# Columns of sc1 and sh1 as one-column products of w_ada's blocks with silu(c)

## The chip, the core and the metric

The kernel runs on one core of a Trainium2 chip. Its time is the device time of one execution in microseconds (us), median of three runs. A core has five engines that run side by side, each working through its own queue in order: PE (matrix products; the load of the stationary operand is shown apart as PEld), DVE (vector), ACT (scalar, activations), POOL and SP, which here only issues DMAs. PE's clock has two levels, 1.2 and 2.4 GHz; the profile shows the granted clock as a share of the higher one.

## What is computed

One layer of a decoder trunk over 2048 tokens of 1024 channels, in float32. The part that the change touches is the modulation at the head of the layer:

```
c_act = silu(c)                                  # 1024 values
mod = c_act @ w_ada[l] + b_ada[l]                # [1024] x [1024, 6144]
sh1, sc1, g1, sh2, sc2, g2 = split(mod, 6)
h = rmsnorm(x, norm_mix_in[l]) * (1.0 + sc1) + sh1
proj = h @ w_in[l]                               # then attention, pooling, gating
```

Everything after it (attention in windows, pooling, spatial gating, output projection and a SwiGLU FFN) depends on h, and so on sc1 and sh1, which take 2 x 1024 columns of w_ada, 8 MB.

## The kernel before

The 2048 tokens go in four groups of 512. Products that need more than the short format of one pass are made of a high and a low part, three passes each (`mm3`, lines of `L90`). Plain float32 operands go through `mm` (also L90), and the compiler makes two instruction pairs (weight load and product) of each such call.

`start()` handles group 0. It normalizes the four token tiles (L379), turns them into channels by transposes on PE (`turn`, L384), and forms sc1 and sh1 by quarters of 256 channels, since w_ada arrives by quarters: `loads(q)` (L399) issues four DMAs of 512 KB for a quarter, two for sh1 (j = 0) and two for sc1 (j = 1), each with 4 of the 8 blocks of 128 input channels. All 16 loads are issued ahead; between them stand the first three strips of w_in (L269). For each quarter:

- DVE makes the weighted sum of the eight blocks for sc1 into `acc` (one L434 and seven L436, each reading a column of `cact`, which is silu(c));
- ACT scales the eight blocks of sh1 in place (L441), POOL adds them up in four steps (L443 to L446);
- PE sums both over the 128 partitions by products with a column of ones: four calls of `mm`, two blocks of 128 channels for each of the two sums, eight instruction pairs;
- DVE adds the bias and forms A = (1 + sc1) * norm and the shift (L453 to L455) from the PSUM tile `aux`, of which there is one buffer;
- ACT applies them to the transposed tokens (L298), DVE splits the result into high and low part (L300, L301), and this is `hT[kc]`, for the two blocks of 128 channels of that quarter;
- PE transposes of quarter q + 2 (they reuse the PSUM banks that L298 has read), and the products of all strips so far with all `hT` so far (`first[j]`, three strips, 72 passes in all).

The block from the weighted sums to `hT` stands under `hp()`, which gives its instructions the priority of instructions 400 places earlier. The order of each engine's queue is set ahead of the run by the planner of the tile framework from priorities and from a timeline that it simulates; on the chip each queue then goes strictly in that order. After `start()`, `proj_a` evicts `first[0..2]` (L489), stores them (L490) and goes on with the rest of the projections; SP's queue carries these stores, the further strips (L269), further w_ada loads (L166) and the tokens of the next group (L148) in one order. Tiles of tag `b` (21 buffers) hold the 16 w_ada tiles, then `hT`; `raw` has 3 buffers, `hl` 4.

Of the kernel before, what the change touches and what calls it, by code (L numbers as in the profile page):

```python
# [12 lines left out]
AF = mybir.ActivationFunctionType  # L13
ALU = mybir.AluOpType

P = 128
T = 2048
D = 1024
KC = D // P
# [17 lines left out]
def tile_hybrid_trunk(  # L37
# [22 lines left out]
    PE, ACT, DVE, POOL, SP = nc.tensor, nc.scalar, nc.vector, nc.gpsimd, nc.sync  # L60
# [27 lines left out]

    def mm(ps, lhsT, rhs, start=True, stop=True):
        PE.matmul(ps, lhsT=lhsT, rhs=rhs, start=start, stop=stop)  # L90

# [8 lines left out]

# [1 line left out]
    q_s = dram.tile([NH * HD, T], F32, name="q_s")  # L102
# [5 lines left out]

# [1 line left out]
    ident = ct("ident", [P, P])  # L110
    make_identity(nc, ident)
    ones = ct("ones", [P, P])
# [18 lines left out]
    def sig_tail(y, e):  # L131
        """e <- log(1 + exp(-|y|)); y <- min(y, 0) - e; y <- exp(y) = sigmoid(y)."""
        ACT.activation(out=e, in_=y, func=AF.Abs)
        ACT.activation(out=e, in_=e, func=AF.Exp, scale=-1.0)
        ACT.activation(out=e, in_=e, func=AF.Ln, bias=1.0)
        DVE.scalar_tensor_tensor(out=y, in0=y, scalar=0.0, in1=e, op0=ALU.min, op1=ALU.subtract)
        ACT.activation(out=y, in_=y, func=AF.Exp)

    cact = ct("cact", [P, 8])
# [15 lines left out]
    r0 = 0  # L155
# [6 lines left out]

# [1 line left out]
    def ada_load(j, k):  # L164
# [55 lines left out]

# [1 line left out]
    sgn = ct("sgn", [P, 256])  # L222
# [28 lines left out]

# [1 line left out]
    cnt = [0]  # L253

    def wsplit(raw, hl):
        """hl[:, 0] + hl[:, 1] = raw, exactly."""
        n = raw.shape[1] * raw.shape[2]
        cnt[0] += 1
        r = raw.rearrange("p a b -> p (a b)")
        h = hl[:, 0].rearrange("p a b -> p (a b)")  # L260
        l = hl[:, 1].rearrange("p a b -> p (a b)")
        with hp():
            ACT.activation(out=h, in_=r, func=AF.Copy)  # L263
            eng = POOL if cnt[0] % 3 == 0 else DVE
            eng.tensor_tensor(out=l, in0=r, in1=h.bitcast(F32), op=ALU.subtract)  # L265
# [38 lines left out]
    def to_channels(xts, A, sh, res):  # L304
        """4 tiles [128 tok, 1024] -> 8 tiles [128 ch, hi/lo, 512 tok] of A * x + sh."""
        pss = {}
        for kc in range(KC):
            with hp():
                if kc % 3 == 2:
                    ps = aux()  # L310
                elif kc % 3 == 0:
                    zt = zps()
                    ps = zt[:, 0]
                else:
                    ps = zt[:, 1]
                for t in range(4):
                    PE.transpose(
                        out=ps[:, t * P : (t + 1) * P], in_=xts[t][:, kc * P : (kc + 1) * P], identity=ident
                    )
                pss[kc] = ps  # L320
                last = [kc] if kc % 3 == 2 else ([kc - 1, kc] if kc % 3 == 1 else [])
                for k in last:
                    res.append(modulate(pss[k], A, sh, k))
            yield

    def ws_unit(ps, hl, hT):
        """weight-stationary: ps[128 out ch, 512 tok]."""
        for kc in range(KC):
            mm3(
                ps, (hl[:, 0, kc, :], hl[:, 1, kc, :]), (hT[kc][:, 0], hT[kc][:, 1]), 0, 0, kc == 0, kc == KC - 1  # L330
            )

    def seg_scale(raws, dim):
        """1/rms over the channels of raws (tiles [128 ch, 512]), on every partition."""
        sqs = []
        for r in raws:
            sq = st("t2", [P, 512])
            ACT.activation(out=sq, in_=r, func=AF.Square)
            sqs.append(sq)
            if len(sqs) == 2:  # L340
                POOL.tensor_tensor(out=sqs[0], in0=sqs[0], in1=sqs[1], op=ALU.add)
                sqs.pop()
        ps = aux()
        mm(ps, ones, sqs[0])
        rs = st("t2", [P, 512])
        ACT.activation(out=rs, in_=ps, func=AF.Ln, scale=1.0 / dim, bias=epst)
        ACT.activation(out=rs, in_=rs, func=AF.Exp, scale=-0.5)
        return rs
# [7 lines left out]

# [1 line left out]
    hTs = {}  # L358
# [13 lines left out]
    first = []  # L372

    def start():
        """h of group 0 and its first products, as sc1 and sh1 become known by quarters of the channels."""
        xts = xt0
# [17 lines left out]
        def loads(q):  # L394
            res = {}
            for j in (0, 1):
                for hf in range(2):
                    wt = st("b", [P, 4, 256])
                    SP.dma_start(  # L399
                        out=wt,  # L400
                        in_=w_ada[0, hf * 512 : (hf + 1) * 512, j * D + q * 256 : j * D + (q + 1) * 256].rearrange(
                            "(k p) c -> p k c", p=P
                        ),
                    )
                    res[j, hf] = wt
            return res
# [10 lines left out]
        raws = []  # L417
# [9 lines left out]
        for q in range(4):  # L427
            w = wq.pop(q)
            with hp():
                acc = w[1, 0][:, 0, :]  # L430
                for k in range(KC):
                    wt = w[1, k // 4][:, k % 4, :]
                    if k == 0:
                        DVE.tensor_scalar(out=acc, in0=wt, scalar1=cact[:, 0:1], scalar2=None, op0=ALU.mult)  # L434
                    else:
                        DVE.scalar_tensor_tensor(  # L436
                            out=acc, in0=wt, scalar=cact[:, k : k + 1], in1=acc, op0=ALU.mult, op1=ALU.add
                        )
                for k in range(KC):
                    wt = w[0, k // 4][:, k % 4, :]  # L440
                    ACT.activation(out=wt, in_=wt, func=AF.Copy, scale=cact[:, k : k + 1])  # L441
                a0, a1 = w[0, 0], w[0, 1]
                POOL.tensor_tensor(out=a0[:, 0:2], in0=a0[:, 0:2], in1=a0[:, 2:4], op=ALU.add)  # L443
                POOL.tensor_tensor(out=a1[:, 0:2], in0=a1[:, 0:2], in1=a1[:, 2:4], op=ALU.add)
                POOL.tensor_tensor(out=a0[:, 0:2], in0=a0[:, 0:2], in1=a1[:, 0:2], op=ALU.add)
                POOL.tensor_tensor(out=a0[:, 0], in0=a0[:, 0], in1=a0[:, 1], op=ALU.add)  # L446
                ps = aux()
                for i, s in enumerate((acc, a0[:, 0])):
                    for cb in range(2):
                        mm(ps[:, 2 * i + cb : 2 * i + cb + 1], s[:, cb * P : (cb + 1) * P], ones[:, 0:1])  # L450
                qs = slice(2 * q, 2 * q + 2)
# [25 lines left out]
    def proj_a(g):  # L477
        tok = slice(g * GT, (g + 1) * GT)
        hT = hTs[g]
        # q, k  # L480
        for j in range(4):
# [10 lines left out]
        for j in range(4):  # L492
# [11 lines left out]
            yield 5.2  # L504
        # v
        for vb in range(2):
            hls = [strip(w_in[0], 1024 + vb * 256, 256, 4 * u, 4) for u in range(2)]
            for tp in range(2):
# [23 lines left out]
                yield 5.2  # L532
        # pooling
        praw = []
# [41 lines left out]

# [1 line left out]
    def proj_b(g, ga):  # L578
# [83 lines left out]

# [1 line left out]
    def att_front(g, h, i, qst, kst, koff):  # L664
        """weights of stick breaking of q tile i (of group g): [128 q, keys]."""
        nk = 5 if g > 0 else i + 1
# [45 lines left out]
    def att_back(g, i0, wq, vst, av):  # L712
        """av[:, pair] += [v_hi | v_lo]^T w^T for q tiles i0, i0 + 1."""
        if g > 0:
# [95 lines left out]

# [1 line left out]
    mTs = {}  # L812
# [35 lines left out]
    def tok_gemm(acts, w, r0, nk, gain, x1):  # L848
        """x1 += gain * (acts^T w[r0 : r0 + nk * 128]); acts: nk tiles [128, hi/lo, 512 tok]."""
        for hf in range(2):  # L850
# [70 lines left out]
    def down(g):  # L921
        f0, n, acts = ACTS.pop(0)
        yield from tok_gemm(acts, w_down[0], f0 * P, n, M["g2"], X1[g])

    def down_last(g):
        """the last part of down() with the final norm of each token tile right after it."""
        f0, n, acts = ACTS.pop(0)
# [59 lines left out]

# [1 line left out]
    att = attention()  # L989
# [14 lines left out]
    def weave(fg, *sides):  # L1004
        """emit fg; each side (generator, first tick, steps per tick[, last tick]) goes along."""
        live = [[e[0], e[1], e[2], 0.0, e[3] if len(e) > 3 else 1000] for e in sides]
# [103 lines left out]
```

## Time and profile before

| | |
|---|---|
| time, median of 3 runs | 2464.58 us (2461.14 to 2466.43) |
| span of the profiled execution | 2463.7 us, 32486 instructions |
| PE busy | 2352.7 us, 95% |
| weight loads (PEld) busy | 1977.3 us, 80% |
| DVE, ACT, POOL busy | 1692.1 (69%), 1362.9 (55%), 1217.0 us (49%) |
| mean granted clock of PE | 0.986 |

The profile gives the profiled execution's span, from its first to its last instruction; its own time is not given apart from the three runs. "Busy" is the time in which an engine has an instruction under way; products overlap one another, so the duration of one is longer than the distance from one start to the next. Times in rows count from the span's start.

### The profile page before, as it was taken

The numbers are of one execution on the slowest core, as the hardware profiler recorded it, in microseconds if no ns is written. First come the engines' busy times: TensorE is split into PE (matmuls) and PEld (weight loads), VectorE is DVE, ScalarE is ACT, GpSimd is POOL, SyncE is SP. The second block draws the span as 40 slices with busy tenths as digits, with TensorE's granted clock in tenths as the row PEclk, the third lists the DMA queues.
The fourth block names the chain that finished last, engine by engine and source line by source line (L and its number), as shares of the span: only waits on it lengthen the run. The fifth ranks groups of instructions, "written<-read, shape, count | busy, mean of one in ns | idle before, by whom it ended". The sixth has DMA issues, their size and how long they took to land.

```text
span 2463.7 us, 32486 instructions
## 1 busy us (share of the span) xinstructions
PE 2352.7 (95%) x11730; PEld 1977.3 (80%) x11730; DVE 1692.1 (69%) x2125; ACT 1362.9 (55%) x2307; POOL 1217.0 (49%) x1157
## 2 busy tenths in 40 slices
PE   5999999999999999998999999889999999999998
PEld 4888979788788888777888888768788878788887
DVE  7577888767876777878877777877775456543435
ACT  5366767656666655656665655566664343433333
POOL 4142533345465455675554555754554456344445
PEclk8999999999999999999999999999999999999999
DMA  8857374554333333433433334334333343433332
GB/s 250 270 167 238 120 244 133 158 165 122 96 97 105 105 104 98 139 121 100 129 115 105 105 102 132 124 98 130 99 103 90 102 146 102 140 95 99 98 100 77
DMA packets 336512, 315.62 MB, mean 128 GB/s; under 512 B 12168, under 2 KB 267870, under 8 KB 336352
## 3 DMA queue, kind: packets, MB, share of 16 engines
q1 hardware_dynamic: 336352, 313.56, 41.3%
q8 instruction: 92, 1.51, 0.2%
q14 instruction: 68, 0.56, 0.1%
HBM read 279.95 MB, written 33.56 MB: 127 GB/s over the span
## 4 chain that ended last, share of the span: by engine, by line
PE 49%; DVE 18%; POOL 11%; issue 10%; ACT 8%; DMA 4%; SPq 1%; POOLq 0%; DVEq 0%; ACTq 0%
PE d L90 45%; POOL b L868 4%; DVE ee L704 3%; DVE hl L265 2%; DVE zc L707 2%; POOL hl L265 2%; PE av L90 2%; ACT hl L263 1%; DMA qst<-q_s 1%; DVE b L301 1%; PE tr L735 1%; DMA b<-in_w_ada_dram 1%; PE z L90 1%; DVE ee L690 1%; POOL b L916 1%
## 5 line engine op out<-in xcount | busy, mean ns | idle before, releaser
L90 PE MATMUL d<-b,hl 128*128 128x512 f32 x5184 | 1254.2, 395 | 8.3 <-DVE b L300 3.2
L90 PEld LDWEIGHTS d<-b,hl 128*128 128x128 f32 x5184 | 961.9, 189 | 208.2 <-DVE b L300 5.0
L90 PE MATMUL d<-hl,b 128*128 128x512 f32 (+1 forms) x4428 | 913.9, 359 | 13.2 <-DVE y L867 12.4
L90 PEld LDWEIGHTS d<-hl,b 128*128 128x128 f32 x4428 | 728.9, 191 | 128.3 <-DVE y L867 15.0
L263 ACT ACTIVATE hl<-raw 128x1024 fp32r<-128x1024 f32 x368 | 387.1, 1054 | 238.0 <-PE d L90 231.0
L265 POOL TENSOR_TENSOR hl<-raw,hl 128x1024 fp32r<-128x1024 f32 x122 | 308.2, 2527 | 325.1 <-ACT hl L263 308.7
L265 DVE TENSOR_TENSOR hl<-raw,hl 128x1024 fp32r<-128x1024 f32 x246 | 336.1, 1368 | 191.9 <-ACT hl L263 185.0
L868 POOL TENSOR_TENSOR b<-b,y 128x512 f32<-128x512 f32 x248 | 388.8, 1576 | 143.4 <-DVE y L867 135.8
L916 POOL TENSOR_TENSOR b<-y,b 128x512 fp32r<-128x512 f32 x88 | 165.0, 1875 | 228.3 <-DVE b L915 223.0
L704 DVE TENSOR_TENSOR_SCAN ee<-ee 128x640 f32<-128x640 f32 (+4 forms) x128 | 204.5, 1598 | 61.8 <-POOL ee L698 54.8
L867 DVE TENSOR_TENSOR y<-d,b 128x512 f32<-128x512 f32 x248 | 167.7, 681 | 91.4 <-PE d L90 88.9
L709 ACT ACTIVATE zc<-zc 128x640 f32<-128x640 f32 (+4 forms) x128 | 85.8, 670 | 257.5 <-POOL zc L698 223.4
L90 PE MATMUL av<-wT,vst 128*128 128x256 f32 x672 | 173.0, 295 | 30.6 <-DVE wT L751 13.4
L693 POOL TENSOR_SCALAR_AFFINE_SELECT zc<-zc 128x128 f32<-128x128 f32 x128 | 81.4, 636 | 221.9 <-DVE zc L707 213.8
L751 DVE TENSOR_TENSOR wT<-tr,wT 128x128 fp32r<-128x128 f32 (+1 forms) x280 | 116.6, 416 | 85.5 <-ACT wT L750 85.2
L90 PEld LDWEIGHTS av<-wT,vst 128*128 128x128 f32 x672 | 122.5, 192 | 59.7 <-DVE wT L751 21.4
L750 ACT ACTIVATE wT<-tr 128x128 fp32r<-128x128 f32 (+1 forms) x280 | 105.8, 378 | 104.4 <-DVE wT L751 71.2
L690 DVE SCALAR_TENSOR_TENSOR ee<-zc,ee 128x640 f32<-128x640 f32 (+4 forms) x128 | 125.5, 981 | 47.9 <-ACT ee L688 47.2
L693 POOL TENSOR_SCALAR_AFFINE_SELECT ee<-ee 128x128 f32<-128x128 f32 x128 | 53.6, 419 | 193.2 <-DVE ee L690 189.6
L907 ACT ACTIVATE y<-d 128x512 f32<-128x512 f32 x88 | 52.3, 594 | 150.8 <-PE d L90 150.7
L707 DVE TENSOR_TENSOR zc<-zc,ee 128x640 f32<-128x640 f32 (+4 forms) x128 | 133.7, 1044 | 2.4
L910 DVE SCALAR_TENSOR_TENSOR y<-d,y 128x512 f32<-128x512 f32 x88 | 60.3, 685 | 84.1 <-ACT y L909 83.7
(187 smaller groups left out, 2248.1 us busy)
## 6 DMA issues: line engine op xcount, KB each, us to landing
raw<-in_w_gate_up_dram SPq DMA_DIRECT2D x176, 512.0 KB, 3.9
raw<-in_w_down_dram SPq DMA_DIRECT2D x88, 512.0 KB, 3.7
raw<-in_w_in_dram SPq DMA_DIRECT2D x72, 512.0 KB, 5.2
b<-in_w_ada_dram SPq DMA_DIRECT2D x48, 512.0 KB, 6.7
raw<-in_w_out_dram SPq DMA_DIRECT2D x32, 512.0 KB, 4.3
b<-in_x_dram SPq DMA_DIRECT2D x28, 512.0 KB, 6.0
kst<-k_s SPq DMA_DIRECT2D x24, 512.0 KB, 4.1
qst<-q_s SPq DMA_DIRECT2D x64, 128.0 KB, 4.3
```

Source lines behind the costliest of these rows:

```text
L90: PE.matmul(ps, lhsT=lhsT, rhs=rhs, start=start, stop=stop)
L263: ACT.activation(out=h, in_=r, func=AF.Copy)
L265: eng.tensor_tensor(out=l, in0=r, in1=h.bitcast(F32), op=ALU.subtract)
L690: DVE.scalar_tensor_tensor(out=sp, in0=zc, scalar=0.0, in1=e, op0=ALU.max, op1=ALU.add)
L693: POOL.affine_select(out=t[:, n - P : n], in_=t[:, n - P : n], pattern=[[-1, P]], compare_op=ALU.is_ge, fill=fill, base=-1, channel_multip ...
L704: DVE.tensor_tensor_scan(out=e[:, ::-1], data0=sp[:, ::-1], data1=sp[:, ::-1], initial=0.0, op0=ALU.add, op1=ALU.bypass)
L707: DVE.tensor_tensor(out=zc, in0=zc, in1=e, op=ALU.subtract)
L750: ACT.activation(out=wT[:, 0, a:b], in_=tr[:, a:b], func=AF.Copy)
L751: DVE.tensor_tensor(out=wT[:, 1, a:b], in0=tr[:, a:b], in1=wT[:, 0, a:b].bitcast(F32), op=ALU.subtract)
L867: DVE.tensor_tensor(out=y, in0=ps, in1=gain[:, cs], op=ALU.mult)
L868: POOL.tensor_tensor(out=x1[t][:, cs], in0=x1[t][:, cs], in1=y, op=ALU.add)
L916: POOL.tensor_tensor(out=a[:, 1], in0=y, in1=a[:, 0].bitcast(F32), op=ALU.subtract)
```

## The change

In place of the weighted sums, PE multiplies each block of w_ada itself (as the stationary operand, 128 input channels by 128 columns) with the matching column of silu(c): per quarter 2 halves x 2 parts x 4 blocks x 2 column blocks = 32 calls of `mm`, all summed in PSUM as one accumulation group over four columns of `aux`. The sums on DVE, ACT and POOL go, and so do the products with ones. The loads of a quarter are issued by halves of the input channels, sc1 first.

```diff
-    def mm(ps, lhsT, rhs, start=True, stop=True):
-        PE.matmul(ps, lhsT=lhsT, rhs=rhs, start=start, stop=stop)
+    def mm(ps, lhsT, rhs, start=True, stop=True, skip=False):
+        PE.matmul(ps, lhsT=lhsT, rhs=rhs, start=start, stop=stop, skip_group_check=skip)
...
-            for j in (0, 1):
-                for hf in range(2):
+            for hf in range(2):
+                for j in (1, 0):
...
-                acc = w[1, 0][:, 0, :]
-                for k in range(KC):
-                    wt = w[1, k // 4][:, k % 4, :]
-                    if k == 0:
-                        DVE.tensor_scalar(out=acc, in0=wt, scalar1=cact[:, 0:1], scalar2=None, op0=ALU.mult)
-                    else:
-                        DVE.scalar_tensor_tensor(
-                            out=acc, in0=wt, scalar=cact[:, k : k + 1], in1=acc, op0=ALU.mult, op1=ALU.add
-                        )
-                for k in range(KC):
-                    wt = w[0, k // 4][:, k % 4, :]
-                    ACT.activation(out=wt, in_=wt, func=AF.Copy, scale=cact[:, k : k + 1])
-                a0, a1 = w[0, 0], w[0, 1]
-                POOL.tensor_tensor(out=a0[:, 0:2], in0=a0[:, 0:2], in1=a0[:, 2:4], op=ALU.add)
-                POOL.tensor_tensor(out=a1[:, 0:2], in0=a1[:, 0:2], in1=a1[:, 2:4], op=ALU.add)
-                POOL.tensor_tensor(out=a0[:, 0:2], in0=a0[:, 0:2], in1=a1[:, 0:2], op=ALU.add)
-                POOL.tensor_tensor(out=a0[:, 0], in0=a0[:, 0], in1=a0[:, 1], op=ALU.add)
                 ps = aux()
-                for i, s in enumerate((acc, a0[:, 0])):
-                    for cb in range(2):
-                        mm(ps[:, 2 * i + cb : 2 * i + cb + 1], s[:, cb * P : (cb + 1) * P], ones[:, 0:1])
+                n = 0
+                for hf in range(2):
+                    for i, j in enumerate((1, 0)):
+                        for k in range(4 * hf, 4 * hf + 4):
+                            for cb in range(2):
+                                n += 1
+                                mm(
+                                    ps[:, 2 * i + cb : 2 * i + cb + 1], w[j, hf][:, k % 4, cb * P : (cb + 1) * P],
+                                    cact[:, k : k + 1], n == 1, n == 32, True,
+                                )
```

## Rows read from the trace of the kernel before

**Rows 1.** The page, 40 slices of the span: busy tenths and granted clock of PE

```profile
PE   5999999999999999998999999889999999999998
PEclk8999999999999999999999999999999999999999
```

**Rows 2.** Busy time by stretch of the opening: us of PE, PEld, DVE, ACT, POOL, clock, DMA

```profile
13.83:22.04 8.21, 0.00 (x1) 0.00 (x0) 5.91 (x9) 4.16 (x9) 4.19 (x4) 1.00 1.11 340
22.04:28.63 6.59, 3.42 (x15) 3.33 (x16) 6.52 (x10) 4.51 (x9) 5.16 (x4) 1.00 1.12 332
28.63:40.23 11.60, 6.93 (x22) 4.70 (x21) 10.30 (x18) 3.96 (x10) 5.92 (x4) 0.78 1.12 335
40.23:51.58 11.35, 10.42 (x41) 7.86 (x41) 11.31 (x17) 6.61 (x13) 9.28 (x9) 0.77 0.59 159
51.58:64.60 13.02, 11.50 (x47) 9.04 (x48) 7.98 (x17) 2.38 (x4) 0.00 (x0) 0.87 0.49 161
```

**Rows 3.** Operations of the first 65 us by line: count, busy, mean ns, idle before

```profile
L90 PE MATMUL d<-b,hl 128*128 128x512 f32 x73 | 24.1, 480 | 3.9 <-DVE hl L265 1.9 <-DVE b L300 1.5 <-DVE b L301 0.5
L441 ACT ACTIVATE b<-b,cact 128x256 f32<-128x256 f32 x32 | 13.3, 496 | 2.5 <-DMA b<-in_w_ada_dram 2.5
L436 DVE SCALAR_TENSOR_TENSOR b<-b,cact,b 128x256 f32<-128x256 f32 x16 | 13.2, 827 | 0.2
L90 PE MATMUL aux<-ones,b 128*128 128x1 f32 x32 | 5.7, 299 | 9.3 <-DVE b L436 8.2 <-issue 1.1
L384 PE MATMUL z<-ident,qst 128*128 128x128 f32 x4 | 1.7, 419 | 0.0
```

**Rows 4.** Timeline of w_ada's loads: when quarter 1 reaches ACT, and the last issue

```profile
20.64 3.30 ACT L441 ACTIVATE b<-b,cact 128x256 f32<-128x256 f32 x8 [0.46 <-DMA b<-in_w_ada_dram]
32.99 0.86 SPq L399 DMA_DIRECT2D b<-in_w_ada_dram  x1
```

**Rows 5.** Timeline of PE: one-column products (start, us), and what follows the last

```profile
22.04 1.87 PE L90 MATMUL aux<-ones,b 128*128 128x1 f32 x8 [8.21 <-DVE b L436]
36.72 1.84 PE L90 MATMUL aux<-ones,b 128*128 128x1 f32 x8 [0.86 <-issue]
47.74 1.02 PE L90 MATMUL aux<-ones,b 128*128 128x1 f32 x8 [0.28 <-issue]
51.58 4.73 PE L90 MATMUL d<-b,hl 128*128 128x512 f32 x18 [0.39 <-DVE b L300]
56.15 0.94 PE L90 MATMUL aux<-ones,b 128*128 128x1 f32 x8
57.46 0.63 PE L243 MATMUL aux<-ident,t 128*128 128x128 f32 x4 [0.36 <-PE aux L90]
59.20 33.15 PE L90 MATMUL d<-b,hl 128*128 128x512 f32 x138 [1.12 <-DVE b L300]
185.25 1.84 PE L90 MATMUL aux<-ones,b 128*128 128x1 f32 x16
```

**Rows 6.** Busy time in steps of 2 us, columns as in rows 2: the clock

```profile
46.00:48.00 2.00, 1.46 (x8) 0.96 (x7) 2.00 (x3) 0.00 (x0) 1.92 (x2) 1.00 0.74 216
...
56.00:58.00 2.00, 1.64 (x14) 1.39 (x12) 0.35 (x3) 0.40 (x1) 0.00 (x0) 1.00 0.28 76
58.00:60.00 2.00, 0.88 (x3) 0.71 (x3) 1.88 (x4) 1.05 (x2) 0.00 (x0) 0.75 1.03 325
60.00:62.00 2.00, 2.00 (x6) 1.54 (x6) 0.71 (x2) 0.00 (x0) 0.00 (x0) 0.50 0.98 274
```

**Rows 7.** Instructions on tile aux, whole span: ns min/median/max, first and last start

```profile
L90 PE MATMUL aux<-ones,b x64: 164/250/374, 22.0 to 317.9; 128*128 128x1 f32 x64
L317 PE MATMUL aux<-ident,b x56: 270/272/329, 125.6 to 2087.1; 128*128 128x128 f32 x56
```

**Rows 8.** Timeline of ACT: the third eviction of the first products

```profile
67.07 0.60 ACT L489 ACTIVATE y<-d 128x512 f32<-128x512 f32 x1
```

**Rows 9.** Who waited for whom, SP's queue, 33 to 130 us: total us, times, longest

```profile
SPq L490 <- ACT y L489: 8.7, 3, 6.9
```

## Prediction

> **What bounds the kernel now.** Start with the page's 40 slices: PE is at nine tenths or more in nearly all of them, except the first, where it is at five [rows 1]. So over the span the kernel is bound by PE, and work added to PE costs its own time, unless it fits where PE waits. The opening is where it waits, and it is the opening that the change rewrites. Then read the opening by stretch [rows 2]: from 13.83 to 64.60 us PE is busy 0.00 + 3.42 + 6.93 + 10.42 + 11.50 = 32.27 of 50.77 us, idle 18.5. In the same rows DVE is close to full from 22.04 to 51.58 and DMA close to full until 40.23. So two things pace the opening: the loads up to about 40 us, and after that the sums on DVE (with ACT and POOL beside it). The operations by line name them [rows 3]: L441 on ACT, 32 in 13.3 us, and L436 on DVE, 16 of whose 28 take 13.2 us. The timeline of PE shows what that does: the one-column products that end a quarter's sums come at 22.04, 36.72, 47.74 and 56.15 [rows 5], though the last load of all is issued at 32.99 [rows 4]. Seen from DVE, the change is right: the sums are late. The question is what it charges to PE.
>
> **The price of a one-column product.** The new operation is in the trace in the same form, though with other data: a 128x128 float32 block as the stationary operand, one moving column. One call of `mm` makes two instruction pairs: four calls a quarter are eight [rows 5]. A quarter's 32 calls will therefore be 64 pairs, 256 for the four quarters. The pace is the distance from start to start, so I take the last one's own duration off the stretch. At 22.04, 8 take 1.87 us, of which the last is some 0.37 (the longest of [rows 7]): (1.87 - 0.37) / 7 = 0.214 us. At 36.72: (1.84 - 0.37) / 7 = 0.210. At 185.25, 16 take 1.84, with the median duration of 0.250: (1.84 - 0.25) / 15 = 0.106 [rows 5, 7]. So there are two prices, a factor of two apart, and they go with PE's clock: 185.25 lies in dense work at the higher level, 36.72 in a stretch whose mean of 0.78 shows that part of it ran at the lower [rows 2].
>
> One trap: the clock column reads 1.00 from 13.83 to 28.63 too [rows 2]. The durations deny it. A 128x128 transpose takes 419 ns there against 272 ns later [rows 3, 7], and the products at 22.04 have the slow price. The opening runs at 1.2 GHz, whatever the column says there. 256 pairs cost 256 x 0.214 = 54.8 us at the lower level and 256 x 0.106 = 27.1 at the higher.
>
> **Which level?** Each quarter becomes some 13.7 us (64 x 0.214) of one-column products. No row shows a stretch of them longer than 2 us, so both levels are open, and they are the ends of the range. I take the lower, for two reasons in rows. The first quarter starts at the lower level anyway. And at 56.15 to 58.1 PE goes from dense work at 1.00 to eight one-column products and four transposes, then waits; although it is busy 1.64 of the 2 us from 56 to 58, the clock falls to 0.5 in the next [rows 5, 6]; whereas it is busy only 1.46 of the 2 us from 46 to 48, with mostly wide products, and stays at 1.00 there [rows 6]. That is weak evidence (one fall, with a wait beside it), but it points to products of one column not holding the clock. The Trainium skill, "TensorE: Matmul & The Clock Gate", Part 1, "What's actually happening", says that throttled is the default and that activity releases it; read plainly, back-to-back products would bring the higher level by themselves, and by that rule the sum below would be that of the first rival.
>
> **The sum, part by part.** It runs from 13.83 us (the first transposes are done) to where the first products end, which is just before the third eviction at 67.07 [rows 8]; after that both kernels have the same work, and PE has no wait from 59.20 to 92.35 [rows 5].
> - Added: 256 pairs, +54.8 us of PE.
> - Removed on PE: the products with ones, 1.87 + 1.84 + 1.02 + 0.94 = 5.7 us [rows 5].
> - Removed on DVE, ACT and POOL: all their sums. They gain nothing by themselves; what they give is the 18.5 us in which PE waited, which the new products can fill: -18.5.
> - New waits: from the last one-column product of a quarter to its first wide product lie bias, L298, L300 and L301, which stay. This took 51.58 - 48.76 = 2.8 us in quarter 2 and 59.20 - 57.09 = 2.1 in quarter 3 [rows 5]. Four such gaps are 8.4 to 11.2 us. The transposes of quarters 2 and 3 fill some, and the planner may put the next quarter's products there: quarter 1 arrives from 20.64 on [rows 4], before quarter 0's products can end. But `aux` is one buffer, so they wait for the bias at least. Between 0 and 8 us; I take 4.
> - Dense work at a better clock: the 72 passes of the first products took about 24.1 us for 73 [rows 3], largely at the lower level. At 59.20, 138 take 33.15, 0.24 each [rows 5]; 72 would be 17.3, if they come in longer runs. Between 0 and -6; I take -4.
> - Products at the better clock: after a dense run the clock is up, and the next quarter's products begin with it. Some 3 us of three quarters at half price would save 9. Between 0 and -9; I take -5.
> - The order of the loads: the same 16 issues of 512 KB, on SP's queue in the same place. Nothing. Quarter 0's sc1 block now comes first, and PE could begin a little before 13.83, between transposes: under 1 us, not counted.
> - Buffers: the w_ada tiles are released by PE's products, later than by the sums before. Who waits: `hT` from the sixth on (five of 21 `b` buffers are free; it needs quarter 0's, long done) and the next w_ada loads on SP, which no one on PE awaits while it is behind. Nothing, and a few us if the loads' delay should come through.
> - The wait that is added: PE's queue now stands in order behind loads (before, DVE and ACT did). For quarters 1 to 3 these have landed by then. Nothing.
>
> Sum: 54.8 - 5.7 - 18.5 + 4 - 4 - 5 = +25.6 us. The first products end near 93 instead of 67 us. What follows is chained to them: SP's stores of q wait for these evictions (8.7 us in three waits [rows 9]) and stand ahead of the next strips and tokens in one queue, so the whole rest moves with them. I let it all pass to the end. The profiled span was 2463.7 us, 0.9 under the median of 2464.58, so the profile is an ordinary run; 2464.6 + 25.6 = **2490 us**. The forecast's own range takes the bounds: 54.8 - 5.7 - 18.5 + 0 - 6 - 9 = +16 to 54.8 - 5.7 - 18.5 + 8 = +39, 2480 to 2503.
>
> **The first rival: the products lift the clock.** Then 27.1 - 5.7 - 18.5 = +2.9, gaps of 0 to 8, and dense work all at the higher level, 0 to -7: -4 to +11, most likely +3, 2468 us. For it: PE would be busy without a break, and breaks stand ahead of the falls seen. Against it: the fall after 58 [rows 6]. Chance 14%.
>
> **The second rival, faster: the products fit into the waits.** Place: PE's 18.5 us idle between 13.83 and 64.60. The price decides: 256p - 5.7 + 4 must be under 18.5, so p under 0.079 us a pair. At a quarter of the higher level's price (0.106 / 4 = 0.027) they would cost 6.8 us, the sums would vanish, and the loads would set the pace: the last is issued at 32.99, quarter 3 could be in at about 41 [rows 2, 4], and its wide products be done near 52 instead of 67: 2450 us. For it: DVE's load is real [rows 2]. Against it: all rows of this form are at 0.106 or above [rows 5]. The Trainium skill, "TensorEngine Tiling (Array Packing)", "Instruction Overhead", gives about 60 cycles for a product of one column, which is an estimate of 0.025 us at 2.4 GHz and of 6.4 us for 256; the trace disagrees by a factor of four, since the load of the stationary block comes on top. Chance 5%.
>
> **The third: it does not show.** That the shift is taken up later (PE idles 5% of the span): it needs a wait that does not move with the first products. 3%, about 2466.
>
> **How the numbers follow.** Forecast 78%, rivals 14, 5 and 3. A measurement of this kernel can tell about 0.2% from no change, 4.9 us, so "same" is 2459.7 to 2469.5. Faster: 5 from the second rival and 2 from the low end of the first, 7%. Same: 7 of the first, 2 of the third, 9%. Slower: 84%. The range of 8 in 10 goes from 2466 (into the first rival) to 2502.
>
> **What would show it.** In the profile after: 256 one-column products (64 a quarter) with a distance of 0.21 us, stretches of some 13 us each; PE nearly full from 14 us on; DVE, ACT and POOL with long idle times before 90 us; the third eviction (L489) near 93 instead of 67.07. Quarters of 7 us and a clock of 1.00 in them mean the first rival. A distance under 0.08 means the second. If that eviction comes near 93 and the end is under 2470, the shift was taken up later, and I was wrong there.

## The result, and the profile after

| | before | after |
|---|---|---|
| time, median | 2464.95 us (2461.14 to 2466.43, 4 runs) | 2483.24 us (2479.86 to 2484.22, 4 runs) |
| ratio to before | | 1.007, 95% interval 1.0051 to 1.0089 |
| span of the profiled execution | 2463.7 us | 2478.1 us (its own time: 2479.86, the lowest of four) |

The change makes the kernel 18.3 us slower; 25.6 were forecast.

The busy times of the opening by stretch, of the kernel after (columns as in [rows 2], whose lines these answer):

```profile
13.83:22.04 8.21, 8.21 (x40) 8.21 (x41) 1.31 (x2) 1.06 (x1) 0.00 (x0) 1.00 1.09 340
22.04:28.63 6.59, 5.16 (x24) 4.75 (x24) 0.55 (x1) 1.06 (x1) 0.00 (x0) 1.00 1.12 332
28.63:40.23 11.60, 10.68 (x51) 10.71 (x51) 3.09 (x8) 2.50 (x3) 2.35 (x1) 1.00 1.10 334
40.23:51.58 11.35, 11.35 (x63) 10.64 (x63) 3.76 (x8) 2.51 (x3) 2.08 (x4) 1.00 0.92 267
51.58:64.60 13.02, 13.02 (x78) 12.34 (x77) 2.50 (x7) 1.45 (x2) 0.00 (x0) 0.74 0.16 65
64.60:92.70 28.10, 28.10 (x129) 24.23 (x129) 8.47 (x12) 5.86 (x8) 2.41 (x1) 0.82 0.23 68
```

DVE's column, the third of the five busy times, says what the change did: DVE, close to full before, is busy for 1.31, 0.55, 3.09, 3.76 and 2.50 us. PE's, the first, says what it cost: in the first five stretches, 50.77 us, PE now waits for only 1.43 + 0.92 us, instead of 18.5. PE's waits were found and filled, and more than filled.

The timeline of PE in the kernel after, its one-column products and the wide products between them (start, us, what):

```profile
11.28 3.55 PE L90 MATMUL aux<-cact,b 128*128 128x1 f32 x16
...
16.43 10.24 PE L90 MATMUL aux<-cact,b 128*128 128x1 f32 x48
...
29.55 13.78 PE L90 MATMUL aux<-cact,b 128*128 128x1 f32 x64 [2.35 <-issue]
...
44.79 3.94 PE L90 MATMUL d<-b,hl 128*128 128x512 f32 x12
48.57 9.00 PE L90 MATMUL aux<-cact,b 128*128 128x1 f32 x64
...
59.02 3.69 PE L90 MATMUL d<-b,hl 128*128 128x512 f32 x12
62.55 9.30 PE L90 MATMUL aux<-cact,b 128*128 128x1 f32 x64
71.72 13.90 PE L90 MATMUL d<-b,hl 128*128 128x512 f32 x48
...
85.81 27.47 PE L90 MATMUL d<-b,hl 128*128 128x512 f32 x120
```

Quarter 0 (3.55 + 10.24 us) and quarter 1 (13.78 us) pay 0.21 us for each of their 64 pairs, the lower clock's price. Quarters 2 and 3 take 9.00 and 9.30, because each begins behind wide products with the clock up and loses it on the way. The clock in steps of 2 us, same kernel (columns as above: PE, PEld, DVE, ACT, POOL, then clock, DMA share and GB/s):

```profile
46.00:48.00 2.00, 2.00 (x8) 1.60 (x8) 1.04 (x3) 1.45 (x2) 0.62 (x3) 1.00 0.53 143
52.00:54.00 2.00, 2.00 (x18) 2.00 (x18) 0.00 (x0) 0.00 (x0) 0.00 (x0) 0.92 0.83 336
54.00:56.00 2.00, 2.00 (x11) 2.00 (x11) 0.00 (x0) 0.00 (x0) 0.00 (x0) 0.50 0.02 6
```

From 52 to 56 both PE and PEld are busy all the time, 2.00 of 2.00, and yet the clock goes from 1.00 to 0.50. So it does not fall for want of work in the queue; it falls while PE does nothing but one-column products. The count beside it, 18 products in the 2 us in which it falls against 11 in the next 2, goes with the two prices.

The third eviction (ACT's copy of a finished product out of PSUM), which stood at 67.07 [rows 8], in ACT's timeline of the kernel after:

```profile
85.80 0.59 ACT L480 ACTIVATE y<-d 128x512 f32<-128x512 f32 x1
```

### The profile page after: what moved, and what is told of

It is laid out like the page before. It is cut to its first block, busy times and chain, and to the rows that moved or that the text cites. A ratio compares the mean times of both kernels' runs of the same rounds, so it can differ in the third digit from the quotient of the medians.

```text
span 2478.1 us, 32834 instructions
## 1 busy us (share of the span) xinstructions
PE 2385.1 (96%) x11954; PEld 2014.6 (81%) x11954; DVE 1669.3 (67%) x2093; ACT 1350.0 (54%) x2275; POOL 1200.1 (48%) x1141
## 4 chain that ended last, share of the span: by engine, by line
PE 49%; DVE 17%; POOL 11%; issue 10%; ACT 8%; DMA 3%; SPq 1%; POOLq 0%; DVEq 0%; ACTq 0%
PE d L90 43%; POOL b L859 4%; DVE ee L695 3%; PE aux L90 2%; DVE zc L698 2%; DVE hl L265 2%; POOL hl L265 2%; PE av L90 1%; ACT hl L263 1%; DVE ee L681 1%; DMA qst<-q_s 1%; POOL zc L684 1%; POOL b L907 1%; DVE b L301 1%; PE tr L726 1%
## 5 line engine op out<-in xcount | busy, mean ns | idle before, releaser
L265 POOL TENSOR_TENSOR hl<-raw,hl 128x1024 fp32r<-128x1024 f32 x122 | 309.3, 2535 | 370.9 <-ACT hl L263 320.8
L265 DVE TENSOR_TENSOR hl<-raw,hl 128x1024 fp32r<-128x1024 f32 x246 | 337.8, 1375 | 205.2 <-ACT hl L263 198.3
```

## The experiments

The theory: a product with one column costs the load of its stationary block, 0.21 us at the lower clock and 0.106 at the higher; such products neither raise nor hold the clock; PE is the bound of the opening once they are on it, and the delay passes to the end. Each time below is compared with the kernel before on the same chip. The edits of the first and the last run are to the kernel before, those of the others to the kernel after, where nothing else is said.

### The order of the loads alone

```diff
-            for j in (0, 1):
-                for hf in range(2):
+            for hf in range(2):
+                for j in (1, 0):
```

> The kernel before with the new order of the loads alone (by halves of the input channels, sc1 first); the sums stay on DVE, ACT and POOL. Theory (the change's cost is PE's one-column products): no difference that can be measured, 2462 to 2468 us, third eviction within 2 us of 67.07. Rival (part of the 18 us comes from the order of the loads, because ACT's part arrives second and POOL ends later): 2468 to 2475 us.

Measured: 2464.35 us against 2462.76, ratio 1.0002 (0.9993 to 1.0010); its third eviction:

```profile
68.40 0.60 ACT L489 ACTIVATE y<-d 128x512 f32<-128x512 f32 x1
```

No difference that can be measured, as expected, while the sums stand. The products with the old order of the loads were not run; nothing here gives the order a share of the loss.

### The same products, 128 columns wide

```diff
+    NW = 128
...
-                                    ps[:, 2 * i + cb : 2 * i + cb + 1], w[j, hf][:, k % 4, cb * P : (cb + 1) * P],
-                                    cact[:, k : k + 1], n == 1, n == 32, True,
+                                    ps[:, (2 * i + cb) * NW : (2 * i + cb + 1) * NW], w[j, hf][:, k % 4, cb * P : (cb + 1) * P],
+                                    cact[:, k : k + 1].to_broadcast([P, NW]), n == 1, n == 32, True,
...
-                DVE.tensor_tensor(out=A, in0=ps[:, 0:2], in1=ba_c[:, KC + 2 * q : KC + 2 * q + 2], op=ALU.add)
+                DVE.tensor_tensor(out=A, in0=ps[:, 0 : 2 * NW : NW], in1=ba_c[:, KC + 2 * q : KC + 2 * q + 2], op=ALU.add)
...
-                DVE.tensor_tensor(out=sh, in0=ps[:, 2:4], in1=ba_c[:, qs], op=ALU.add)
+                DVE.tensor_tensor(out=sh, in0=ps[:, 2 * NW : 4 * NW : NW], in1=ba_c[:, qs], op=ALU.add)
```

> The changed kernel with each product 128 columns wide instead of one (the same column of silu(c) repeated, its results side by side, of which one column is read). The loads of the stationary blocks are the same 256, the work streamed through PE is 128 times as much. Theory (a product costs the load of its block, 0.21 us at the lower and 0.106 at the higher clock, and products of one column neither raise nor hold the clock): the clock rises within the first or second quarter and stays, quarters of 7 us instead of 9.0 to 13.8, third eviction near 70 instead of 85.8, time 2464 to 2472 us. Rival 1 (the price is that of the load in the opening, whatever the clock): no change, 2480 to 2486 us. Rival 2 (wider products cost their columns): slower than the changed kernel, 2490 us or more.

Measured: 2461.42 us, ratio to before 0.9992 (0.9983 to 1.0001), where the changed kernel stands at 1.0070. Its timeline of PE:

```profile
11.40 3.75 PE L90 MATMUL aux<-cact,b 128*128 128x128 f32 x16 [0.20 <-DMA b<-in_w_ada_dram]
...
16.66 5.52 PE L90 MATMUL aux<-cact,b 128*128 128x128 f32 x48
...
22.60 7.38 PE L90 MATMUL aux<-cact,b 128*128 128x128 f32 x64 [0.20 <-PE av_s L385]
...
33.47 7.30 PE L90 MATMUL aux<-cact,b 128*128 128x128 f32 x64
...
44.90 7.30 PE L90 MATMUL aux<-cact,b 128*128 128x128 f32 x64
```

and its third eviction in ACT's:

```profile
63.71 0.60 ACT L481 ACTIVATE y<-d 128x512 f32<-128x512 f32 x1
```

The same 256 loads of the same blocks, with 128 times as many columns behind each, take 3.75 + 5.52 + 7.38 + 7.30 + 7.30 = 31.3 us instead of 45.9. From the second stretch on a pair costs some 0.11 us, and no quarter falls back. At either clock a pair costs the same with 128 columns as with one: from start to start 0.213 us in the first stretch and 0.112 later, the two values that the one-column pairs of the kernel after have too. This decides it: the price was the clock's, the clock was lost to the one column, and 128 columns cost nothing visible. That the load of the block sets this price is not shown by itself; the rows of PEld are full in these stretches in both kernels. The gain, 22 us of eviction time, is more than was expected (70 was, 63.71 it is; and the time lies 2.6 us under the 2464 to 2472 expected): besides the 14.6 us of the products, the 72 wide products now run at the higher clock and take 17.5 us instead of 21.5 (3.02 + 3.66 + 6.42 + 4.38, same timeline), and the transposes run faster too.

### Each product twice

```diff
+    chalf = ct("chalf", [P, 8])
+    DVE.tensor_scalar(out=chalf, in0=cact, scalar1=0.5, scalar2=None, op0=ALU.mult)
...
-                            for cb in range(2):
+                            for cb in (0, 1, 0, 1):
...
-                                    cact[:, k : k + 1], n == 1, n == 32, True,
+                                    chalf[:, k : k + 1], n == 1, n == 64, True,
```

> The changed kernel with each one-column product done twice, with half of silu(c): 512 pairs instead of 256. Theory (0.21 us a pair in stretches of such products, all on PE's path, and the delay passes to the end): about 256 x 0.2 = 51 us more than the changed kernel, third eviction near 135, time 2525 to 2540 us. Rival (a pair costs 0.106 in long stretches and the rest of the 18 us is waits for loads and gaps): 27 us more or less, 2505 to 2512 us. If the delay were partly taken up later, the end moves less than the third eviction does.

Measured: 2538.21 us against 2462.76, ratio 1.0303 (1.0287 to 1.0318): 75.5 us above before, where the changed kernel stood 18.3 above its own before, so 57.2 us more. Its timelines of PE and, last line, of ACT:

```profile
11.84 27.44 PE L90 MATMUL aux<-chalf,b 128*128 128x1 f32 x128 [0.38 <-DVE vst L381]
...
41.30 27.30 PE L90 MATMUL aux<-chalf,b 128*128 128x1 f32 x128
...
74.78 24.81 PE L90 MATMUL aux<-chalf,b 128*128 128x1 f32 x128
...
105.64 24.93 PE L90 MATMUL aux<-chalf,b 128*128 128x1 f32 x128
...
144.18 0.60 ACT L482 ACTIVATE y<-d 128x512 f32<-128x512 f32 x1
```

The products take 104.5 us, 58.6 more than in the changed kernel, 7.6 more than the 51 expected: 0.229 us for each added pair, so none came at the higher clock's price. The third eviction, expected near 135, moves by 144.18 - 85.80 = 58.4, the end by 57.2. The second 27 us stretch is 0.213 us a pair from its first to its last: two stretches of 27 us without a break in them did not bring the higher clock. And nearly all of a further delay in the opening reaches the end.

### sc1 on PE, sh1 on ACT and POOL

```diff
+                for k in range(KC):
+                    wt = w[0, k // 4][:, k % 4, :]
+                    ACT.activation(out=wt, in_=wt, func=AF.Copy, scale=cact[:, k : k + 1])
+                a0, a1 = w[0, 0], w[0, 1]
+                POOL.tensor_tensor(out=a0[:, 0:2], in0=a0[:, 0:2], in1=a0[:, 2:4], op=ALU.add)
...
-                    for i, j in enumerate((1, 0)):
-                        for k in range(4 * hf, 4 * hf + 4):
...
+                    for k in range(4 * hf, 4 * hf + 4):
...
+                                ps[:, cb : cb + 1], w[1, hf][:, k % 4, cb * P : (cb + 1) * P],
+                                cact[:, k : k + 1], n == 1, False, True,
...
+                for cb in range(2):
+                    mm(
+                        ps[:, 2 + cb : 3 + cb], a0[:, 0, cb * P : (cb + 1) * P], ones[:, 0:1], False, cb == 1, True,
+                    )
```

> One half of the change: sc1 by one-column products (DVE's sums are gone), sh1 by ACT and POOL as before, summed over partitions by products with ones: 144 pairs instead of 256 (before: 32). Theory (PE pays 0.214 a pair at the lower clock, 30.8 - 5.7, against 18.5 us of waits that DVE's sums caused): +3 to +12 us against before, 2467 to 2476 us. Rival (relief of DVE is worth more than PE's price, as long as the products are few): faster than before, 2450 to 2460 us.

Measured: 2460.52 us against 2462.76, ratio 0.9986 (0.9976 to 0.9997). Neither expectation holds: the time is well under 2467 to 2476, and barely under that of before. Its products of sc1 in quarters 1 to 3, and ACT's third eviction:

```profile
25.46 6.96 PE L90 MATMUL aux<-cact,b 128*128 128x1 f32 x32 [0.36 <-PE aux L90]
...
39.69 4.95 PE L90 MATMUL aux<-cact,b 128*128 128x1 f32 x32
...
52.91 4.55 PE L90 MATMUL aux<-cact,b 128*128 128x1 f32 x32
...
69.62 0.60 ACT L491 ACTIVATE y<-d 128x512 f32<-128x512 f32 x1
```

With the 3.55 and 3.41 us of quarter 0 the products take 23.4 us against the 18.5 us of waits: the eviction is 2.5 us later than before, a little under the 3 to 12 expected of the whole, but the end is not. A few us of delay at this place are taken up behind it (below); a gain of 0.1% is at the edge of what can be told.

### The two together: sc1 on PE, 128 columns wide

```diff
-                                ps[:, cb : cb + 1], w[1, hf][:, k % 4, cb * P : (cb + 1) * P],
-                                cact[:, k : k + 1], n == 1, False, True,
+                                ps[:, cb * NW : (cb + 1) * NW], w[1, hf][:, k % 4, cb * P : (cb + 1) * P],
+                                cact[:, k : k + 1].to_broadcast([P, NW]), n == 1, False, True,
```

(against the run before it; `NW` is 128 as above, and the reads of `ps` follow)

> sc1 by products of PE as in the changed kernel, but 128 columns wide, and sh1 by ACT and POOL as before: what the two runs before it gained, put together. PE has 128 pairs at 0.106 (13.6 us) and 16 with ones. Theory (PE's price at the higher clock is under the 18.5 us of waits that DVE's sums caused, so the opening gets shorter): third eviction at 58 to 63 us instead of 67.07, and 2 to 6 us off the whole, 2457 to 2461 us. Rival (the chain on ACT and POOL, some 8.5 us a quarter, takes the place of DVE's): eviction at 65 or later and no difference from before, 2462 to 2465 us. Second rival (what the opening gains is lost again in the waits for the next group's tokens at 92 to 104 us): eviction early and the time still within 2 us of before.

Measured: 2458.5 us against 2462.41, ratio 0.9980 (0.9972 to 0.9989), the fastest of the complete kernels: 3.9 us under before. Its products in quarters 1 to 3, and ACT's third eviction:

```profile
25.29 6.14 PE L90 MATMUL aux<-cact,b 128*128 128x128 f32 x32 [0.36 <-PE aux L90]
...
35.77 3.81 PE L90 MATMUL aux<-cact,b 128*128 128x128 f32 x32 [0.36 <-PE aux L90]
...
48.02 3.81 PE L90 MATMUL aux<-cact,b 128*128 128x128 f32 x32 [0.37 <-PE aux L90]
...
62.95 0.60 ACT L492 ACTIVATE y<-d 128x512 f32<-128x512 f32 x1
```

The eviction is 4.1 us earlier than before, and the end 3.9: both within what the theory gave (58 to 63, 2457 to 2461), the eviction at the end of the smaller gain.

### No sums at all

```diff
-                acc = w[1, 0][:, 0, :]
-                for k in range(KC):
...
-                POOL.tensor_tensor(out=a0[:, 0], in0=a0[:, 0], in1=a0[:, 1], op=ALU.add)
+                acc, a0 = w[1, 0][:, 0, :], w[0, 0]
```

> The kernel before with the sums left out: each quarter's products with ones read one unscaled block of w_ada for sc1 and one for sh1, so sc1 and sh1 are not what the reference has; all loads, products with ones and everything after them stay. It shows what the opening is worth if sc1 and sh1 cost nothing but their loads. Theory (the loads pace the opening up to about 41 us): third eviction at 50 to 56 us, 11 to 17 us ahead of before. If that passes to the end as the delays did (55 of 58 us): 2447 to 2453 us. Rival (an early opening meets the waits for the next group's tokens at 92 to 104 us and is lost there): 2457 to 2463 us, and then no way of forming sc1 and sh1 could bring much.

Measured: 2452.4 us against 2462.41, ratio 0.9958 (0.9944 to 0.9971), 10.0 us. The third eviction:

```profile
57.48 0.60 ACT L473 ACTIVATE y<-d 128x512 f32<-128x512 f32 x1
```

It comes 9.6 us earlier, 1.5 us later than the expected 50 to 56, and all of it reaches the end within the interval (7 to 14 us). Not all of PE's waits go with the sums; busy times from 13.83 to this kernel's first eviction:

```profile
13.83:54.60 40.77, 30.84 (x123) 24.84 (x122) 15.99 (x33) 9.81 (x12) 3.38 (x5) 0.96 0.96 290
```

PE still waits 9.9 us. So this opening, with its order of transposes, splits and wide products, has about 10 us to give to any way of forming sc1 and sh1. The changed kernel paid 45.9 us on PE for it.

## Why the prediction was right, point by point

**The bound, and the price by clock.** Right, and shown. A pair costs 0.21 at the lower and 0.11 at the higher clock, in stretches of up to 128 pairs; two of the four quarters took some 13.8 us, as forecast, two 9.0 and 9.3. (At the higher clock the pairs stand 0.112 us apart; the prediction's 0.106 took in the first gap of a stretch, which is shorter, 0.026.) The run with 128 columns and that with doubled products tell the clock from the number of columns, from waits for loads and from gaps.

**The first rival** (the products lift the clock by themselves) fell: 27.30 us of products, back to back, all at 0.213. The Trainium skill, "TensorE: Matmul & The Clock Gate", Part 1, "What's actually happening", puts the clock down to how busy PE is; the trace disagrees if one-column products with a full queue of weight loads are taken for busy, and agrees with 128 columns. **The second** (products cheap enough to fit) was not met by any row: no stretch of this form has a pace under 0.1 us a pair. By the Trainium skill, "TensorEngine Tiling (Array Packing)", "Instruction Overhead", the 256 would take 6.4 us, an estimate; they took 45.9.

**The size.** The forecast was +25.6; the end moved by 18.3. Term by term, at PE:
- Products: 54.8 - 5 = 49.8 forecast, 3.55 + 10.24 + 13.78 + 9.00 + 9.30 = 45.9 measured. The term for products at the better clock was mis-sized: 54.8 - 45.9 = 8.9, at the end of the bound (0 to 9), where 5 were taken. It came from two quarters (4.7 and 4.4 us under the 13.7 of a quarter at the lower clock), not from three.
- Waits filled: 18.5 less 4 of gaps forecast. PE's idle time in the same 50.77 us is 2.35, one gap, so 16.2 are filled. The transposes of later quarters and the next products cover the other gaps.
- Wide products at the better clock: 4 forecast. 72 now take 3.94 + 3.69 + 13.90 = 21.5 against 24.1 for 73 [rows 3]: 2.6.
- Sum: 45.9 - 5.7 - 16.2 - 2.6 = +21.4.

The traces have that to half a us. The wide products after the first ones are the same 120, and their stretch ends at 59.20 + 33.15 = 92.35 before [rows 5] and at 85.81 + 27.47 = 113.28 after: +20.9. The eviction moved by 18.7 only, because before it came late: the 120 take 27.47 us after, so the first ones of before had ended near 92.35 - 27.5 = 64.9, an estimate, 2 us ahead of the third eviction; after, they end 0.2 us ahead of it (71.72 + 13.90 = 85.62). The mark chosen for the sum, 67.07, was ACT's and not PE's, and hid 2 us.

**What passes to the end.** The forecast let all of it pass. Behind the stretch of 120, PE waits for the next group's tokens. Before:

```profile
94.63 0.33 PE L317 MATMUL z<-ident,b 128*128 128x128 f32 x1 [1.92 <-DVE b L365]
...
103.64 0.48 PE L317 MATMUL z<-ident,b 128*128 128x128 f32 x1 [3.54 <-DVE b L365]
...
114.04 0.71 PE L317 MATMUL z<-ident,b 128*128 128x128 f32 x5
```

After:

```profile
114.75 0.33 PE L317 MATMUL z<-ident,b 128*128 128x128 f32 x1 [1.35 <-DVE b L365]
...
120.32 0.33 PE L317 MATMUL z<-ident,b 128*128 128x128 f32 x1 [0.94 <-DVE b L365]
...
127.64 0.33 PE L317 MATMUL z<-ident,b 128*128 128x128 f32 x1 [0.76 <-DVE b L365]
...
130.91 0.71 PE L317 MATMUL z<-ident,b 128*128 128x128 f32 x5
```

The first wait, the second and the five transposes moved by 20.1, 16.7 and 16.9 us. The second wait shrinks from 3.54 to 0.94, and the clock, which before fell during it (the transpose of 0.48 us is one at the lower clock), stays up; a third wait of 0.76 comes in its place. So about 4 us of the delay are taken up here: what the third rival held for unlikely as a whole happened in part, and the step that failed is "I let it all pass to the end".

Where nearly half of it lies, POOL's and DVE's timelines show. Before:

```profile
100.70 2.34 POOL L265 TENSOR_TENSOR hl<-raw,hl 128x1024 fp32r<-128x1024 f32 x1 [20.05 <-ACT hl L263]
101.18 2.41 DVE L365 TENSOR_SCALAR b<-b,sm 128x1024 f32<-128x1024 f32 x1
```

After:

```profile
119.51 0.75 DVE L365 TENSOR_SCALAR b<-b,sm 128x1024 f32<-128x1024 f32 x1
120.20 2.40 POOL L265 TENSOR_TENSOR hl<-raw,hl 128x1024 fp32r<-128x1024 f32 x1 [19.18 <-ACT hl L263]
```

L365 scales the tokens that PE waits for. Before, POOL's split begins ahead of it, and it takes 2.41 us; after, it goes first and takes 0.75. So some 1.7 us were not time to spare, but a collision that the kernel before has and the kernel after does not. The other traces divide in the same way: 2.47 and 2.79 us behind POOL's split in the run with sc1 128 columns wide and in that without sums, 0.75 ahead of it in the other four. No run varied this order alone. The half change, 2.5 us late at the eviction, belongs to those four, and at the five transposes it is 0.4 us ahead of before (114.04):

```profile
113.59 0.71 PE L317 MATMUL z<-ident,b 128*128 128x128 f32 x5
```

From 16.9 at the last mark to 18.3 at the end there is no cause to name: the two profiled spans differ by 14.4, and the runs of after spread over 4.4 us.

**The removals on DVE, ACT and POOL** were costed at nothing beyond PE's waits, and the run without sums agrees: with PE free of the products their absence is worth 10 us, no more. The sums were not behind all of the 18.5 us of waits; 9.9 us stay without them. **The order of the loads** was costed at nothing; measured 1.0002, with the sums in place. The smaller bookings (buffers, the wait behind loads) were not tried one by one; the idle time of 2.35 us leaves them little room. One reading set a span beside times: the profiled span of after is 1.8 us under the time of the same execution (2478.1 and 2479.86), so the profiled execution of before took some 2465.5 us (an estimate), 0.9 above the median and not under it; it is an ordinary run all the same.

## What to carry to other kernels

An engine that waits is not an engine with time to spare: compare the price of the moved work at the clock that the engine will have there with the waits it can fill, here 45.9 us against 18.5. Products of one column cost as much as products of 128 and lost the clock as well; where they can't be avoided, repeat the column so that the product is wide (31.3 instead of 45.9 us for the same loads), and leave on the other engines the part that they do in time. Before moving work, measure the opening without it: its 10 us were about the most that a version with this order could win, and the best one here won 3.9. And a wait far behind the change can hold a collision that a shift undoes, so a delay read at one place is not yet the delay of the end.

## What the runs showed of the hardware

- Width behind a weight load was free up to 128 columns: 64 pairs of 128 columns take 7.30 us, 0.112 from start to start, as the one-column pairs at the higher clock; at the lower clock both stand 0.213 apart.
- The clock fell while PE's product and weight-load rows both read full (52 to 56 us of the kernel after), and did not rise in 27 us of such work. In these traces a full row of busy time was no sign of the clock that the work got.
- The profile's clock column reads 1.00 at the start of every kernel here, while the durations (transposes of 419 ns against 272 [rows 3, 7]) show the lower clock: in an opening, read durations.
- The same DVE instruction (L365, 128 x 1024) took 2.41, 2.47 and 2.79 us in the three traces where a split of POOL (L265) began ahead of it, and 0.75 in the five where it went first.
